# Strassen's seven half products in the MLP up projection of a fused decoder layer

## The chip, the cores and the metric

The kernel runs on one core of a Trainium2 chip. The core has five engines that the profile names PE (TensorE: matrix products), DVE (VectorE), ACT (ScalarE), POOL (GpSimd) and SP (SyncE, which here only issues DMAs). Each engine executes its own queue strictly in order; engines wait for each other by semaphores. The metric is the device time of one execution in microseconds (us). Three runs of the kernel before gave 668.95, 668.95 and 672.06 us.

## The reference

One decoder layer on a sequence of 512 tokens of width 1024, in float32: a mixer of two attention groups, then a squared-ReLU MLP with a hidden width of 4096, then a final RMSNorm. The change concerns the MLP alone:

```python
D_MODEL = 1024; SEQ = 512; D_FF = 4 * D_MODEL

def squared_relu_mlp(h, w_up, w_down):
    return jnp.square(jax.nn.relu(h @ w_up)) @ w_down

        h = h + squared_relu_mlp(rmsnorm(h, g_mlp[l]), w_up[l], w_down[l])
    return rmsnorm(h, g_final)
```

## The kernel before

A float32 product is made of three TensorE products of TensorE's 32-bit type fp32r. Each operand x is split into a high half xh (an fp32r copy, made on ACT) and a low half xl = x - xh (a subtraction on DVE); the function `mm3` (L189 to L192) then issues `lh*rh`, `ll*rh` and `lh*rl` into the same PSUM bank. The first operand of a matmul is the stationary one (a 128x128 block, loaded ahead by LDWEIGHTS, which the profile calls PEld), the second is the moving one. The printed rows name the moving one and then the stationary one: `S<-uh,wh` multiplies moving `uh` into stationary `wh` and adds into PSUM tile `S`. The PSUM tiles that the MLP uses are called S, T, O and acc.

The MLP input, normalised but for its row scale, lies transposed in SBUF as `uh`/`ul` (8 row blocks `kt` of 128 features, 512 tokens each). The 4096 hidden features are worked off in 8 blocks, e = 0 to 7, of 512 features, each in two halves:

- Up half: for each of four groups f of 128 features, `up_mm` (L1071) issues 8 kt x 3 = 24 matmuls that move 512 columns (tokens), so 96 in all. After each group follow a ReLU on ACT into `mt` (L1139), a square on ACT into the fp32r tile `ah` (L1140), the same square in full precision on POOL into `ma` (L1141), and `al = ma - ah` on DVE (L1142).
- Down half: for each of the four token groups tb and two column halves, 4 f x 3 = 12 matmuls of 512 columns, 96 in all. Stationary are blocks of `ah`/`al`, moving are the down weights. DVE adds each result to the residual `h1` (L1156). In the first token group (tb = 0) the groups f are taken as (0, 1, 2) for both column halves and then (3,).

The weights come from DRAM in pieces of 512 KB (128x1024, tile `wr`), issued by SP, and are split by `Ring`: ACT copies `wh` (L164), DVE subtracts `wl` (L118). Two sets of buffers exist: `ring`, whose tiles lie at the upper end of SBUF and are 512 wide, and `ring2`, at the lower end, 1024 wide; of each nine pieces three go to `ring` and six to `ring2`, so a projection's operands lie partly at one end and partly at the other. The right-hand pools put, counted in bytes of a partition, `uh`/`ul` at 143K and 160K, `h1` at 180K, `ring`'s halves at 204K to 229K; on the left lie `ring2`'s halves (35K to 84K) and `ah`/`al` (88K to 121K).

In block e = 0 three of the four up groups are begun early, while the last transposes of the input (`mlp_in`, four of them) are still being made. POOL has nothing else to do there.

The order of PE's queue is that of the code. The order on ACT, DVE, POOL and SP is laid down ahead of the run by a list scheduler over the whole program; on the chip it is fixed.

Of the kernel before, what the change touches and what calls it, by code (L numbers as in the profile page):

```python
# [15 lines left out]
P = 128  # L16
D = 1024
# [36 lines left out]
def hybrid_layer(tc, x, xT, wp, wfg, cst, gfin, out):  # L54
# [134 lines left out]
    def mm3(ps, lh, ll, rh, rl, first, last):  # L189
        nc.tensor.matmul(ps, lh, rh, start=first, stop=False)  # L190
        nc.tensor.matmul(ps, ll, rh, start=False, stop=False)  # L191
        nc.tensor.matmul(ps, lh, rl, start=False, stop=last)  # L192
# [855 lines left out]
    close_pool("att", "foxv")  # L1048
    hp = open_pool("hp", "right")
    h1 = hp.tile([P, NT, D], F32, name="h1")  # L1050
    ssh = cp.tile([P, NT, 2], F32, name="ssh")
    up = open_pool("up", "right")
    uh = up.tile([P, NK, S], F32R, name="uh")
    ul = up.tile([P, NK, S], F32R, name="ul")

    def wout_evac(ps, tb, half):
        cols = slice(512 * half, 512 * half + 512)
        nc.vector.scalar_tensor_tensor(h1[:, tb, cols], ps, rf[:, tb:tb + 1], fc["xr"][:, tb, cols], op0=ALU.mult, op1=ALU.add)
        jk = up.tile([P, S], F32, tag="jk", name=nm("jk"), bufs=2)
        nc.scalar.activation(jk, h1[:, tb, cols], AF.Square, accum_out=ssh[:, tb, half:half + 1])  # L1060
# [50 lines left out]
    gfb = mp.tile([P, D], F32, name="gfb")  # L1111
    nc.sync.dma_start(gfb, gfin.to_broadcast([P, D]))
# [10 lines left out]
    def nbank():  # L1123
        un[0] += 1
        return bank(tags[un[0] % 8])

    for e in range(8):
        ah = mp.tile([P, 4, S], F32R, tag="ah", name=nm("ah"), bufs=2)
        al = mp.tile([P, 4, S], F32R, tag="al", name=nm("al"), bufs=2)
        for f in range(4):  # L1130
            if early:
                w, ps = early.pop(0)
                up_mm(ps, w, range(4, NK))
            else:
                w, ps = mlp_piece(), nbank()
                up_mm(ps, w, range(NK))
            t = mp.tile([P, S], F32, tag="mt", name=nm("mt"), bufs=2)
            a = mp.tile([P, S], F32, tag="ma", name=nm("ma"), bufs=2)
            nc.scalar.activation(t, ps, AF.Relu)  # L1139
            nc.scalar.activation(ah[:, f, :], t, AF.Square)  # L1140
            nc.gpsimd.tensor_tensor(a, t, t, op=ALU.mult)  # L1141
            nc.vector.tensor_sub(al[:, f, :], a, f32(ah[:, f, :]))  # L1142
        wd = [mlp_piece() for _ in range(4)]
        for tb in range(NT):
# [35 lines left out]
    close_pool("up", "hp", "ringA", "edge", "mp", "ring2", "cp")  # L1180


def _pieces(w_in, w1k, w1v, w_out, w_up, w_down):
# [97 lines left out]
```

## Time and profile before

| | us |
|---|---|
| three runs | 668.95, 668.95, 672.06 |
| median | 668.95 |
| profiled execution | 669.01 |
| its span, first to last instruction | 667.2 |
| PE busy in the span | 650.7 (98%) |
| DVE busy | 405.6 (61%) |
| ACT busy | 312.8 (47%) |
| POOL busy | 170.6 (26%) |

The profiled execution is within 0.1 us of the median, and 1.8 us of it lie outside the span. Matmuls are pipelined: a row of 512 columns has a duration of about 0.39 us, but the next starts some 0.23 us later, so a step is read from start to start. The up half of block 0 begins, in part, at 306 us, its down half at 330.13 us, and the last matmul of the MLP starts at 659.76 us. Block 1 onwards fills the stretch from 352 to 660 us.

### The profile page before, as it was taken

How to read it: one execution, taken by the hardware profiler on the slowest of the kernel's cores; microseconds unless marked ns; L12 is line 12 of the kernel's file. 1: busy time of each engine (PE TensorE's matmuls, PEld its weight loads, DVE VectorE, ACT ScalarE, POOL GpSimd, SP SyncE). 2: the span in 40 equal slices, each digit the busy share in tenths (PEclk: the TensorE clock that was granted, in tenths of full speed). 3: DMA queues.
4: the chain of work that ended last, by engine and by line, in shares of the span. 5: the costliest groups of instructions: out<-in, count | busy, mean ns of one | idle time of the engine just before them, and what ended most of it. 6: DMA issues, size and time to landing. Idle time of an engine off the chain costs nothing.

```text
span 667.2 us, 9167 instructions
## 1 busy us (share of the span) xinstructions
PE 650.7 (98%) x3165; PEld 535.6 (80%) x3165; DVE 405.6 (61%) x872; ACT 312.8 (47%) x673; POOL 170.6 (26%) x203
## 2 busy tenths in 40 slices
PE   9998999999999999999999999999999999999995
PEld 7767888878787878888888888888888888888884
DVE  4798887868866789847936344354344433544146
ACT  5435536777867878637704223143142340422222
POOL 0262062655756745200301101001011020010121
PEclk9999999999999999999999999999999999999999
DMA  7723610000022573225814214143051330401002
GB/s 273 232 96 127 213 71 33 2 33 32 32 88 65 146 219 88 71 88 168 292 45 164 90 58 157 38 150 104 1 190 63 107 114 32 158 1 32 0 33 94
DMA packets 22878, 66.72 MB, mean 100 GB/s; under 512 B 4272, under 2 KB 4912, under 8 KB 22832
## 3 DMA queue, kind: packets, MB, share of 16 engines
q1 hardware_dynamic: 22688, 66.10, 29.4%
q8 instruction: 25, 0.41, 0.2%
q14 instruction: 21, 0.17, 0.1%
q10 hardware_dynamic: 144, 0.04, 0.0%
HBM read 59.81 MB, written 2.10 MB: 93 GB/s over the span
## 4 chain that ended last, share of the span: by engine, by line
PE 86%; DVE 8%; issue 2%; DMA 2%; ACT 1%; SPq 0%; POOL 0%; DVEq 0%; ACTq 0%
PE S L192 8%; PE S L190 8%; PE S L191 8%; PE acc L190 6%; PE acc L192 6%; PE acc L191 6%; PE O L190 5%; PE O L192 5%; PE O L191 5%; PE T L190 5%; PE T L192 5%; PE T L191 5%; PE O L756 4%; PE T L738 4%; PE S L710 2%
## 5 line engine op out<-in xcount | busy, mean ns | idle before, releaser
L164 ACT ACTIVATE wh<-wr 128x512 fp32r<-128x512 f32 (+1 forms) x144 | 103.5, 743 | 157.6 <-PE O L191 59.0
L118 DVE TENSOR_TENSOR wl<-wr,wh 128x512 fp32r<-128x512 f32 (+1 forms) x126 | 119.9, 971 | 93.5 <-ACT wh L164 91.6
L1141 POOL TENSOR_TENSOR ma<-mt 128x512 f32<-128x512 f32 x32 | 35.7, 1115 | 326.7 <-ACT mt L1139 326.7
L720 ACT ACTIVATE sp<-sp,st 128x128 f32<-128x128 f32 (+1 forms) x96 | 53.2, 555 | 16.9 <-DVE st L718 16.4
L718 DVE CUSTOM_DVE_ANT_0 sp<-S,c 128x128 f32<-128x128 f32 (+1 forms) x96 | 43.0, 485 | 18.7 <-PE S L711 18.2
L726 POOL TENSOR_SCALAR sp<-sp,st,gt 128x128 f32<-128x128 f32 (+1 forms) x64 | 38.5, 614 | 47.0 <-ACT sp L720 26.7
L118 DVE TENSOR_TENSOR ptl<-T,pth 128x128 fp32r<-128x128 f32 (+1 forms) x96 | 44.3, 483 | 2.9 <-ACT pth L748 2.5
L748 ACT ACTIVATE pth<-T 128x128 fp32r<-128x128 f32 (+1 forms) x96 | 38.5, 426 | 9.8 <-PE T L738 9.2
L738 PE MATMUL T<-c,sp 128*128 128x128 f32 x240 | 38.4, 273 | 3.1 <-DVE st L724 1.9
L738 PEld LDWEIGHTS T<-c,sp 128*128 128x128 f32 x240 | 29.6, 140 | 13.1 <-issue 5.1
L190 PE MATMUL S<-wh,ah 128*128 128x512 f32 (+1 forms) x100 | 38.9, 389 | 0.0
L192 PE MATMUL S<-wl,ah 128*128 128x512 f32 (+1 forms) x100 | 38.7, 387 | 0.0
L191 PE MATMUL S<-wh,al 128*128 128x512 f32 (+1 forms) x100 | 38.6, 386 | 0.0
L1156 DVE SCALAR_TENSOR_TENSOR h<-S,r2s,h 128x512 f32<-128x512 f32 (+1 forms) x25 | 18.5, 740 | 32.7 <-PE S L192 32.7
L190 PE MATMUL S<-uh,wh 128*128 128x512 f32 x88 | 34.6, 394 | 0.0
L192 PE MATMUL S<-ul,wh 128*128 128x512 f32 x88 | 34.4, 391 | 0.0
L191 PE MATMUL S<-uh,wl 128*128 128x512 f32 x88 | 34.2, 389 | 0.0
L1142 DVE TENSOR_TENSOR al<-ma,ah 128x512 fp32r<-128x512 f32 x32 | 21.8, 682 | 19.4 <-POOL ma L1141 19.4
L190 PE MATMUL acc<-xh,wh 128*128 128x512 f32 x72 | 30.9, 430 | 0.0
L192 PE MATMUL acc<-xl,wh 128*128 128x512 f32 x72 | 28.5, 395 | 0.0
L191 PE MATMUL acc<-xh,wl 128*128 128x512 f32 x72 | 28.4, 395 | 0.0
L190 PE MATMUL O<-uh,wh 128*128 128x512 f32 x72 | 28.4, 394 | 0.0
(349 smaller groups left out, 1690.3 us busy)
## 6 DMA issues: line engine op xcount, KB each, us to landing
wr<-wp_d SPq DMA_DIRECT2D x91, 512.0 KB, 3.7
wx<-wp_d SPq DMA_DIRECT2D x10, 512.0 KB, 4.2
xr<-x_d SPq DMA_DIRECT2D x4, 512.0 KB, 7.3
out_d<-ob SPq DMA_DIRECT2D x8, 256.0 KB, 2.1
xr<-xT_d SPq DMA_DIRECT2D x3, 512.0 KB, 6.6
fq<-tqh SPq DMA_DIRECT2D x8, 128.0 KB, 4.0
fq<-tq SPq DMA_DIRECT2D x8, 128.0 KB, 3.4
f2q<-tqh SPq DMA_DIRECT2D x8, 128.0 KB, 3.1
```

Source lines behind the costliest of these rows:

```text
L118: eng.tensor_tensor(o, a, b, op=ALU.subtract)
L164: high = lambda: nc.scalar.activation(hi, raw[:, c], AF.Copy)
L190: nc.tensor.matmul(ps, lh, rh, start=first, stop=False)
L191: nc.tensor.matmul(ps, ll, rh, start=False, stop=False)
L192: nc.tensor.matmul(ps, lh, rl, start=False, stop=last)
L718: nc.vector.tensor_tensor_reduce(out=self.p[i], in0=self.ps[i], in1=self.bias(i), scale=1.0, scalar=1e35, op0=ALU.add, op1=ALU.min, accum_ ...
L720: nc.scalar.activation(self.p[i], self.p[i], AF.Exp, bias=m, scale=-1.0, accum_out=den)
L726: nc.gpsimd.tensor_scalar(self.p[i], self.p[i], rs, g, op0=ALU.mult, op1=ALU.mult)
L738: nc.tensor.transpose(pt[:, j * P:j * P + P], self.p[i][:, j * P:j * P + P], ident)
L748: nc.scalar.activation(self.blocks(self.th, i), self.pt[i], AF.Copy)
L756: nc.tensor.matmul(o[:, j * P:S], self.v(j), t[:, 4 * j * P:(3 * j + NT) * P], start=first and part == 0 and j == 0, stop=last and part == ...
L1141: nc.gpsimd.tensor_tensor(a, t, t, op=ALU.mult)
```

## The change

Blocks e = 1 to 7 compute the up half in another way. The weight block W of 1024x512 is seen as 2x2 quarters: a11 and a12 belong to the hidden groups f = 0 and 2, a21 and a22 to f = 1 and 3; the second index is the half of the 1024 input features. The input is seen as 2x2 quarters too: u11, u12 (first 512 features, tokens 0 to 255 and 256 to 511), u21, u22. Instead of eight quarter products, seven are made, of sums of quarters (Strassen's scheme in Winograd's form):

P1 = a11 u11, P2 = (a21+a22)(u12-u11), P3 = (a21+a22-a11)(u22-u12+u11), P4 = a12 u21, P5 = (a11-a21)(u22-u12), P6 = (a12-(a21+a22-a11)) u22, P7 = a22 (u21-(u22-u12+u11)), the last two with their quarters as the kernel stores them.

Each product takes 2 x 4 x 3 = 24 matmuls of 256 columns, so a block has 168 of 256 columns where there were 96 of 512. P1, P3, P5 and P7 accumulate in one bank; ACT copies what stands in it after P1 (`e1`) and after P3 (`ev`), and P2 (`w5`); DVE adds three times (L1210). The weight sums (L1219 and three subtractions) are made on DVE, 1024 wide. The seven factors are then split in halves 512 wide, all in `ring`'s buffers (six of `wh`, six of `wl`: three products).

The four sums of the input are made once, in block 0 (`input_sums`, four calls, code placed in its down half): per call two additions of 512 columns and two subtractions of 256 on POOL (L1153, L118), two subtractions of 256 and two splits on DVE, two copies on ACT (L1159, L1162). They go to `tqh`/`tql`, and the fourth overwrites columns 256 to 511 of `uh`/`ul`.

Further: `ah`/`al` have one buffer in place of two; in the down half's first token group the groups f are taken as (0, 2) and then (1, 3); the down weights all come from `ring2` (four buffers, split 1024 wide), the up weights all from `ring`; the right-hand pools are opened in another order. As a result `uh` lies at 139K, `ul` at 155K, `tqh` and `tql` at 172K and 184K, `ring` at 204K to 229K, and `h1` at 123K; `ring2`'s halves at 52K to 84K, `ah` at 84.6K and `al` at 92.8K. The number of DMAs and their size stay as they were. In block 7 `gfb` and `ob` use raw weight tiles.

The diff, cut to its core:

```diff
-    hp = open_pool("hp", "right")
-    h1 = hp.tile([P, NT, D], F32, name="h1")
     up = open_pool("up", "right")
     uh = up.tile([P, NK, S], F32R, name="uh")
     ul = up.tile([P, NK, S], F32R, name="ul")
+    tqh = up.tile([P, 4, 3, 256], F32R, name="tqh")
+    tql = up.tile([P, 4, 3, 256], F32R, name="tql")
+    hp = open_pool("hp", "right")
+    h1 = hp.tile([P, NT, D], F32, name="h1")
...
-    ring2 = Ring(r2p, 6, 3, 1)
-    def mlp_piece():
-        return (ring if next_piece[0] % 9 < 3 else ring2).piece()
+    ring2 = Ring(r2p, 4, 7, 1)
...
+    def split2(r):
+        w = ([], [])
+        for k in range(2):
+            c = slice(512 * k, 512 * k + 512)
+            hi = rp.tile([P, 512], F32R, tag="wh", name=nm("wh"), bufs=6)
+            lo = rp.tile([P, 512], F32R, tag="wl", name=nm("wl"), bufs=6)
+            nc.scalar.activation(hi, r[:, c], AF.Copy)
+            sub(nc.vector, lo, r[:, c], f32(hi))
...
+    def input_sums(j):
+        r = raw().rearrange("p (k t) -> p k t", k=2)
+        t = raw().rearrange("p (a t) -> p a t", a=4)
+        for k in range(2):
+            nc.gpsimd.tensor_tensor(r[:, k], f32(uh[:, j + 4 * k, :]), f32(ul[:, j + 4 * k, :]), op=ALU.add)
+        u11, u12, u21, u22 = r[:, 0, 0:256], r[:, 0, 256:512], r[:, 1, 0:256], r[:, 1, 256:512]
+        sub(nc.gpsimd, t[:, 0], u12, u11)
+        sub(nc.gpsimd, t[:, 1], u22, t[:, 0])
+        sub(nc.vector, t[:, 2], u22, u12)
+        sub(nc.vector, t[:, 3], u21, t[:, 1])
+        nc.scalar.activation(tqh[:, j], t[:, 0:3], AF.Copy)
+        sub(nc.vector, tql[:, j], t[:, 0:3], f32(tqh[:, j]))
+        nc.scalar.activation(uh[:, j, 256:512], t[:, 3], AF.Copy)
+        sub(nc.vector, ul[:, j, 256:512], t[:, 3], f32(uh[:, j, 256:512]))
...
+    def product(ps, w, moving, first):
+        for p in range(2):
+            for j in range(4):
+                c = slice(P * j, P * j + P)
+                mm3(ps[:, 256 * p:256 * p + 256], w[0][p][:, c], w[1][p][:, c], moving(0, j), moving(1, j),
+                    first and p == j == 0, p == 1 and j == 3, skip_group_check=True)
...
-        ah = mp.tile([P, 4, S], F32R, tag="ah", name=nm("ah"), bufs=2)
-        al = mp.tile([P, 4, S], F32R, tag="al", name=nm("al"), bufs=2)
+        ah = mp.tile([P, 4, S], F32R, tag="ah", name=nm("ah"))
+        al = mp.tile([P, 4, S], F32R, tag="al", name=nm("al"))
...
+            product(pa, split2(a11), lambda h, j: u_in(h, j, 0), True)
+            e1 = half_copy("e1", pa)
+            a21, a22 = up_raw(), up_raw()
+            s1 = raw()
+            nc.vector.tensor_tensor(s1, a21, a22, op=ALU.add)
+            product(pd, split2(s1), lambda h, j: (tqh, tql)[h][:, j, 0], True)
+            w5 = half_copy("w5", pd)
+            sub(nc.vector, s1, s1, a11)
+            product(pa, split2(s1), lambda h, j: (tqh, tql)[h][:, j, 1], False)
+            ev = half_copy("ev", pa)
+            a12 = up_raw()
+            product(pc, split2(a12), lambda h, j: u_in(h, j + 4, 0), True)
+            hidden(ah, al, at(0, 0), add(pc, e1))
+            sub(nc.vector, a21, a11, a21)
+            product(pa, split2(a21), lambda h, j: (tqh, tql)[h][:, j, 2], False)
+            hidden(ah, al, at(1, 1), add(pa, w5))
+            sub(nc.vector, s1, a12, s1)
+            product(pd, split2(s1), lambda h, j: u_in(h, j + 4, 1), False)
+            hidden(ah, al, at(0, 1), add(pd, ev))
+            product(pa, split2(a22), lambda h, j: u_in(h, j, 1), False)
+            hidden(ah, al, at(1, 0), pa)
-        wd = [mlp_piece() for _ in range(4)]
+        wd = [ring2.piece() for _ in range(4)]
...
-            for fs in ((0, 1, 2), (3,)) if tb == 0 else ((0, 1, 2, 3),):
+            for fs in ((0, 2), (1, 3)) if tb == 0 else ((0, 1, 2, 3),):
...
+            if e == 0:
+                input_sums(tb)
```

What the scheduler makes of it is seen at three places. The first is POOL's whole queue around block 0. Before, after an instruction of the attention (`sq`), the four squares of block 0 stand alone:

```order
L783 TENSOR_TENSOR sq_3445<-sq_3445,sq_3294 128x512
L1141 TENSOR_TENSOR ma_3852<-mt_3851 128x512
L1141 TENSOR_TENSOR ma_3870<-mt_3869 128x512
L1141 TENSOR_TENSOR ma_3888<-mt_3887 128x512
L1141 TENSOR_TENSOR ma_3925<-mt_3924 128x512
```

In the changed kernel (`wr_...` are raw tiles that hold the sums, L1187 are the squares; eleven more sums stand above the first row):

```order
L118 TENSOR_TENSOR wr_4057<-wr_4056 128x256
L118 TENSOR_TENSOR wr_4057<-wr_4056,wr_4057 128x256
L1153 TENSOR_TENSOR wr_4096<-uh,ul 128x512
L1187 TENSOR_TENSOR ma_3844<-mt_3843 128x512
L1153 TENSOR_TENSOR wr_4096<-uh,ul 128x512
L118 TENSOR_TENSOR wr_4097<-wr_4096 128x256
L118 TENSOR_TENSOR wr_4097<-wr_4096,wr_4097 128x256
L1187 TENSOR_TENSOR ma_3862<-mt_3861 128x512
L1187 TENSOR_TENSOR ma_3880<-mt_3879 128x512
L1187 TENSOR_TENSOR ma_3921<-mt_3920 128x512
```

All sixteen sums of the input now stand ahead of the second, third and fourth square of block 0, thirteen of them ahead of the first too. The second place is DVE at the end of block 2's up half (`us` are the additions to a product, `wl` low halves of weights, `al` those of the hidden features). Before:

```order
L1142 TENSOR_TENSOR al_4365<-ma_4402,ah_4364 128x512
L118 TENSOR_TENSOR wl_4745<-wr_4742,wh_4744 128x512
L118 TENSOR_TENSOR wl_4749<-wr_4742,wh_4748 128x512
L1142 TENSOR_TENSOR al_4365<-ma_4443,ah_4364 128x512
L118 TENSOR_TENSOR wl_4786<-wr_4783,wh_4785 128x512
L118 TENSOR_TENSOR wl_4790<-wr_4783,wh_4789 128x512
L1142 TENSOR_TENSOR al_4365<-ma_4484,ah_4364 128x512
L118 TENSOR_TENSOR wl_4827<-wr_4824,wh_4826 128x1024
L1142 TENSOR_TENSOR al_4365<-ma_4521,ah_4364 128x512
L1156 SCALAR_TENSOR_TENSOR h_3566<-T_4550,r2s,h_3566 128x512
```

In the changed kernel:

```order
L1210 TENSOR_TENSOR us_4715<-O_4526,w_968_4602 128x512
L118 TENSOR_TENSOR wl_4949<-wr_4942,wh_4948 128x512
L118 TENSOR_TENSOR wl_4985<-wr_4982,wh_4984 128x512
L1210 TENSOR_TENSOR us_4756<-S_4527,ev_4637 128x512
L118 TENSOR_TENSOR al_4525<-ma_4718,ah_4524 128x2x256
L118 TENSOR_TENSOR wl_4989<-wr_4982,wh_4988 128x512
L118 TENSOR_TENSOR wr_4982<-wr_4982,wr_4942 128x1024
L118 TENSOR_TENSOR al_4525<-ma_4759,ah_4524 128x2x256
L118 TENSOR_TENSOR wl_5020<-wr_4982,wh_5019 128x512
L118 TENSOR_TENSOR al_4525<-ma_4797,ah_4524 128x2x256
```

Six rows of the next block's weights (P1 to P3 of block 3: `wr_4942` is its a11, `wr_4982` its sum) now stand between the additions and the low halves of this block's hidden features; the last `al` has the first of P3's `wl` directly ahead of it. The third place is PE where a down half begins (block 3 in the changed kernel, block 2 in the one before; the numbers of `wh` count the groups f in steps of 6, so that 4528 is f = 0 and 4546 f = 3, and 5218 and 5236 likewise). Before, from its 16th matmul on:

```order
L190 MATMUL S_4551<-wh_4540,ah_4364 128x512
L191 MATMUL S_4551<-wh_4540,al_4365 128x512
L192 MATMUL S_4551<-wl_4541,ah_4364 128x512
L190 MATMUL T_4550<-wh_4546,ah_4364 128x512
L191 MATMUL T_4550<-wh_4546,al_4365 128x512
L192 MATMUL T_4550<-wl_4547,ah_4364 128x512
```

In the changed kernel, from its 10th on:

```order
L190 MATMUL acc_5241<-wh_5230,ah_4938 128x512
L191 MATMUL acc_5241<-wh_5230,al_4939 128x512
L192 MATMUL acc_5241<-wl_5231,ah_4938 128x512
L190 MATMUL S_5240<-wh_5224,ah_4938 128x512
L191 MATMUL S_5240<-wh_5224,al_4939 128x512
L192 MATMUL S_5240<-wl_5225,ah_4938 128x512
L190 MATMUL S_5240<-wh_5236,ah_4938 128x512
L191 MATMUL S_5240<-wh_5236,al_4939 128x512
```

Before, the group that is made last, f = 3, is used from the 19th matmul of the down half on. Now f = 0 and 2 fill the first 12 matmuls, and f = 1 and 3 are used from the 13th and the 16th on; their first 256 tokens are what P7, the last product, completes.

## Rows read from the trace of the kernel before

**Rows 1.** The page: engines' busy time, and the granted clock by fortieths of the span.

```profile
PE 650.7 (98%) x3165; PEld 535.6 (80%) x3165; DVE 405.6 (61%) x872; ACT 312.8 (47%) x673; POOL 170.6 (26%) x203
PEclk9999999999999999999999999999999999999999
```

**Rows 2.** The page: the chain that ended last, shares by engine.

```profile
PE 86%; DVE 8%; issue 2%; DMA 2%; ACT 1%; SPq 0%; POOL 0%; DVEq 0%; ACTq 0%
```

**Rows 3.** By windows: us; busy PE, PEld, DVE, ACT, POOL; clock; DMA share, GB/s.

```profile
480.00:520.00 40.00, 40.00 (x176) 32.81 (x175) 18.23 (x21) 12.69 (x18) 4.17 (x4) 1.00 0.31 105
```

**Rows 4.** Timeline of PE (start, duration, us): first matmuls of up and down halves.

```profile
330.13 0.39 PE L190 MATMUL T<-wh,ah 128*128 128x512 f32 x1
...
352.26 0.39 PE L190 MATMUL T<-uh,wh 128*128 128x512 f32 x1
...
374.14 0.39 PE L190 MATMUL S<-wh,ah 128*128 128x512 f32 x1
...
395.91 0.39 PE L190 MATMUL S<-uh,wh 128*128 128x512 f32 x1
...
505.06 0.39 PE L190 MATMUL T<-wh,ah 128*128 128x512 f32 x1
...
527.25 0.40 PE L190 MATMUL T<-uh,wh 128*128 128x512 f32 x1
...
615.55 0.40 PE L190 MATMUL T<-uh,wh 128*128 128x512 f32 x1
...
637.53 0.40 PE L190 MATMUL S<-wh,ah 128*128 128x512 f32 x1
```

**Rows 5.** Timeline of PE at the MLP's end: 512 columns, then 256.

```profile
649.82 0.40 PE L192 MATMUL T<-wl,ah 128*128 128x512 f32 x1
...
657.02 0.28 PE L190 MATMUL O<-wh,ah 128*128 128x256 f32 x1
...
659.76 0.28 PE L192 MATMUL S<-wl,ah 128*128 128x256 f32 x1
```

**Rows 6.** Timeline of weight loads under the steps of 256 columns.

```profile
657.14 0.19 PEld L192 LDWEIGHTS O<-wl,ah 128*128 128x128 f32 x1
657.26 0.19 PEld L190 LDWEIGHTS O<-wh,ah 128*128 128x128 f32 x1
```

**Rows 7.** Lines by form, DVE, 470 to 660 us: count; busy, mean ns; idle before.

```profile
L118 DVE TENSOR_TENSOR wl<-wr,wh 128x1024 fp32r<-128x1024 f32 x18 | 21.8, 1223 | 33.8 <-ACT wh L164 33.8
L1142 DVE TENSOR_TENSOR al<-ma,ah 128x512 fp32r<-128x512 f32 x16 | 11.0, 685 | 19.4 <-POOL ma L1141 19.4
L1156 DVE SCALAR_TENSOR_TENSOR h<-S,r2s,h 128x512 f32<-128x512 f32 x14 | 10.5, 750 | 17.6 <-PE S L192 17.6
```

**Rows 8.** Lines by form, ACT, the same stretch.

```profile
L164 ACT ACTIVATE wh<-wr 128x1024 fp32r<-128x1024 f32 x18 | 18.5, 1052 | 20.5 <-PE O L191 17.8 <-DMA wr<-wp_d 2.6
L1139 ACT ACTIVATE mt<-S 128x512 f32<-128x512 f32 x6 | 3.6, 599 | 19.0 <-PE S L192 19.0
```

**Rows 9.** Timeline of POOL and DVE where one meets the other's work.

```profile
500.56 1.04 POOL L1141 TENSOR_TENSOR ma<-mt 128x512 f32<-128x512 f32 x1 [4.41 <-ACT mt L1139]
501.03 1.12 DVE L118 TENSOR_TENSOR wl<-wr,wh 128x512 fp32r<-128x512 f32 x1 [2.57 <-ACT wh L164]
502.07 0.68 DVE L1142 TENSOR_TENSOR al<-ma,ah 128x512 fp32r<-128x512 f32 x1
...
326.61 2.03 POOL L1141 TENSOR_TENSOR ma<-mt 128x512 f32<-128x512 f32 x1 [1.16 <-ACT mt L1139]
326.53 2.66 DVE L118 TENSOR_TENSOR wl<-wr,wh 128x1024 fp32r<-128x1024 f32 x2
```

**Rows 10.** Lines by form, POOL, whole span: operations with two tiles as operands.

```profile
L783 POOL TENSOR_TENSOR sq<-sq,sq 128x512 f32<-128x512 f32 x4 | 5.2, 1291 | 2.2 <-ACT sq L778 2.2
L670 POOL TENSOR_TENSOR cs<-cs,cm 128x256 f32<-128x256 f32 x4 | 2.8, 710 | 1.2 <-DVE cm L669 1.1
```

**Rows 11.** Timeline of DVE: the fifth of the input's eight low halves.

```profile
310.49 0.75 DVE L1067 SCALAR_TENSOR_TENSOR ul<-T,c,uh 128x512 fp32r<-128x512 f32 x1 [0.72 <-ACT uh L1066]
```

More of the change, by code (lines that the diff above doesn't have):

```diff
@@ L187, in part, with mm3 @@
         return w[0][k][:, c:c + n], w[1][k][:, c:c + n]
[L189 to L192, printed above, removed]
+    def mm3(ps, lh, ll, rh, rl, first, last, **kw):
+        nc.tensor.matmul(ps, lh, rh, start=first, stop=False, **kw)
+        nc.tensor.matmul(ps, ll, rh, start=False, stop=False, **kw)
+        nc.tensor.matmul(ps, lh, rl, start=False, stop=last, **kw)
     def rsqrt(ss, scale, n, rname):
@@ L1125, in nbank, with raw @@
         return bank(tags[un[0] % 8])
-    for e in range(8):
-        ah = mp.tile([P, 4, S], F32R, tag="ah", name=nm("ah"), bufs=2)
-        al = mp.tile([P, 4, S], F32R, tag="al", name=nm("al"), bufs=2)
[L1130 to L1142, printed above, removed]
-        wd = [mlp_piece() for _ in range(4)]
+    def raw():
+        return r2p.tile([P, 1024], F32, tag="wr", name=nm("wr"), bufs=7)
@@ new lines, in u_in, with half_copy @@
+    def u_in(h, j, half):
+        return (uh, ul)[h][:, j, 256 * half:256 * half + 256]
+    def product(ps, w, moving, first):
[4 more added lines that the diff above has]
+                    first and p == j == 0, p == 1 and j == 3, skip_group_check=True)
+    def half_copy(n, ps):
+        t = mp.tile([P, S], F32, tag=n, name=nm(n))
+        nc.scalar.activation(t, ps, AF.Copy)
+        return t
@@ L1151, in hybrid_layer @@
                         mm3(ps, ah[:, f, tok], al[:, f, tok], *part(wd[f], c, n), f == 0, f == 3)
+            if e == 0:
+                input_sums(tb)
             last = groups[-1]
-            ob = mp.tile([P, D], F32, tag="ob", name=nm("ob"), bufs=2) if e == 7 else None
+            ob = raw() if e == 7 else None
+            if e == 7 and tb == 0:
+                gfb = raw()
+                nc.sync.dma_start(gfb, gfin.to_broadcast([P, D]))
             for i, (ps, (c, n)) in enumerate(zip(pss, groups)):
@@ L1206, in _pieces @@
     for e in range(8):
-        for f in range(4):
-            c = (4 * e + f) * P
-            ps += kmajor(w_up[:, c:c + P])
+        up = [kmajor(w_up[:, (4 * e + f) * P:(4 * e + f + 1) * P])[0] for f in range(4)]
+        if e > 0:
+            up = [np.concatenate([up[i][:, 512 * k:512 * k + 512], up[i + 2][:, 512 * k:512 * k + 512]], 1)
+                  for i, k in ((0, 0), (1, 0), (1, 1), (0, 1))]
+        ps += up
         ps += [w_down[(4 * e + f) * P:(4 * e + f + 1) * P] for f in range(4)]
```

47 lines of the change are left out of this document (39 added, 8 removed).

## The prediction

> **What bounds the kernel now.** I read the page first: PE is busy for 650.7 of 667.2 us at the full clock (a 9 in every slice) [rows 1], and the chain that ended last is PE for 86% [rows 2]. By windows, a stretch of the MLP shows it pure: in 40 us PE is never idle, DVE works 18.2 us, ACT 12.7, POOL 4.2 [rows 3]. So in the MLP time is the number of matmul steps times their length, as long as nobody is late; and DVE, the busiest helper, has more than half of its time free. The third view is PE's timeline. An up half takes 21.88 us (352.26 to 374.14) or 21.98 (615.55 to 637.53), a down half 21.77 (374.14 to 395.91) or 22.19 (505.06 to 527.25) [rows 4]; with 96 steps each that is 227 to 231 ns a step. Steps of 256 columns stand at the end: 23 of them from 657.02 to 659.76 are 119.1 ns each, against 232.3 for the 31 steps of 512 before them (649.82 to 657.02) [rows 5]. Half the width costs 51%, so nearly no fixed price hangs on a step.
>
> **The products.** Seven blocks give up 96 steps of 512 and get 168 of 256. At 119.1 ns that is 20.0 us against 21.9: 1.9 less. The same tiles that read 119.1 read 232.3 at 512, 2% above the 228 of an up half, so I scale to 118.5: 19.9 us, 2.0 less, **-14.0 us** in seven blocks (with 119.5 it is -12.8; with 117, half of 228 and 3 ns, -15.7). PE's own work lies on the path, so this counts in full where PE doesn't wait.
>
> What a page says against it: by the Trainium skill, "TensorE: Matmul & The Clock Gate", section "The mechanism" of Part 3, a weight load overlaps a running matmul only where the two use different row groups of the array, and here all use all 128 rows. In the trace two loads of 0.19 us start 0.12 us apart while the matmuls keep their 119 ns [rows 6]; so the trace disagrees. By the page the added loads would be paid, and the sum would be that of the last rival.
>
> **The placement.** Two kinds of down half stand in the trace: 21.77 us in block 1, but 22.13 in block 0 (330.13 to 352.26) and 22.19 in block 4 [rows 4]. What differs is in which buffers the weights lie. With all down weights beside `ah`/`al` I expect the short kind, about 0.4 less in two to three of seven blocks, **-1.0 us**. The bounds are the same 0.4 either way in most blocks, -2.0 to +1.0: that the new places are the better ones no row shows.
>
> **Block 0, which now makes the input's sums.** Before, POOL has only four squares there. Now thirteen of sixteen sums stand ahead of the first square and three ahead of the second. The second addition needs the fifth low half, done at 310.49 + 0.75 = 311.2 [rows 11]. From there to the second square's start POOL has 7 additions (1.29), 8 subtractions (at most 0.71) [rows 10] and a square (1.04 alone [rows 9]): 15.7 us, so about 327.0. The rest goes through three engines in order. POOL's second square ends at 328.1; DVE makes `al` of f = 1 (0.69 [rows 7]) and the subtractions that its queue holds behind it (estimate 0.35 each, half of 512 columns), 329.4; ACT copies a sum of 768 columns (estimate 0.8, between 0.6 for 512 and 1.05 for 1024 [rows 8]) before the ReLU of f = 2 (0.60 [rows 8]), 330.8; POOL's square 331.9, `al` 332.6. The down half starts at 330.13 [rows 4] and, in the new order, wants `al` of f = 2 at its 5th matmul, 331.0: 1.6 late. Then the ReLU of f = 3 waits on ACT behind four copies of 256 columns, one of 768 and two high halves of 512, and its `al` on DVE behind three low halves of 256, one of 768, two of weights and a weight sum: some 4 us, so 336.9 against a need at 333.8 (the 17th matmul). **+3.1 us**, if POOL and DVE don't disturb each other.
>
> But they do. A subtraction of 512 columns that met POOL's square took 1.12 us in place of 0.69, and a square that met DVE's 1024-wide subtractions took 2.03 in place of 1.04 [rows 9]. If half of the sixteen operations ahead of the second square meet one, at up to 1.0 each, up to 8 us more; DVE is occupied about half of this stretch by operations on SBUF, the additions being longer than a square. I take 3 more: **+6.1 us** (1 to 11; no gain, since before nothing waited there).
>
> **The six full blocks after it.** The down half now wants f = 1 at its 13th matmul, so 12 x 0.227 = 2.7 us after its start, 22.6 us after the block's. Two chains end there. The short one begins at P7's end: ReLU 0.1 + 0.6, square 1.04 + 0.07, `al` 0.69: 2.5 us, it would just do. The other is DVE's queue. From the first down weight it lists, up to that `al`: 7 operations of 1024 (four `wl` of down weights, three weight sums), 17 of 512 in SBUF (13 `wl`, 4 `al`), 4 that read PSUM. Following each other they take 0.08 less than their durations (502.07 against 501.03 + 1.12 [rows 9]): 7 x 1.14 + 17 x 0.61 + 4 x 0.67 [rows 7, 9] = 21.1. The first can start 0.9 us before the block does: its buffer's last reader is nine steps from the down half's end (-2.0), and ACT's copy takes 1.05 [rows 8]. So there are 23.5 us. Four meetings with POOL's squares at 0.43 (1.12 less 0.69 [rows 9]) make 22.8, and waits for high halves come on top, since ACT can make a `wh` only when PE has left a buffer: two or three of 0.5, half a copy of 1.05 [rows 8], say 1.4. That is 24.2, 0.7 late. The last `al` also stands behind a `wl` of the next block, whose `wh` waits for a 1024-wide sum two rows above. I take 0.7 a block, six blocks (behind block 7 no weights follow): **+4.2 us** (0 to 1.5 each, 0 to 9). Who waits: PE alone, and all the down half behind it.
>
> **Nothing for the rest.** The DMAs are as many and as large. P7's start and the additions wait for DVE within the chain above. Block 7's `gfb` is loaded later but used only after the first down sums. The tail behind 659.76 keeps its instructions. Two buffers of `ah` become one: P4 writes it after the down half before has ended long since.
>
> **Sum**, on the profiled execution of 669.0 us (0.1 above the median): -14.0 - 1.0 + 6.1 + 4.2 = -4.7, **664.3 us**.
>
> **The rivals.**
> *Meetings cost little* (0.25). What speaks for it: only 0.43 us were lost on DVE in the one meeting [rows 9], and the queues may find room for it. Then block 0 costs 3.1 and the others at most 0.1: 669.0 - 15.0 + 3.1 + 0.6 = 657.7; with the lowest prices 655.
> *The gain is eaten* (0.18). POOL and DVE exclude each other: at 501.03 DVE ran for 1.12 us of which the first 0.43 lie within POOL's square, as if it had waited for its end, and POOL's 2.03 fits a wait for one 1024-wide operation [rows 9]. If so throughout, block 0 costs about 9 and each later block 1.0: 669.0 - 15.0 + 9 + 6 = 669.0, no change. The Trainium skill, "SBUF — State Buffer", section "SBUF: two separate sides", has this as a rule: the port pair that VectorE and GpSimd share is an exclusive lock, held for a whole instruction, when a VectorE instruction with two SBUF inputs meets a GpSimd one that reads SBUF. The first meeting agrees with it (1.12 us); the last only in part, since DVE's two operations there took 2.66 us, 0.3 more than 1.22 + 1.14, where a whole square of 1.04 would have been due.
> *DVE becomes the bound of the up half* (0.09). The up half shrinks by 2 us while DVE's list grows to 21 us of 23.5. It decides from 2.3 us of waiting per block on: then six blocks lose what they gained. For it speaks that each `wl` waits for ACT's `wh` and ACT's queue mixes ReLUs, copies and the next block's halves in fixed order: two or three more waits of a whole copy (1.05) are 2.6 us on top of 0.7: 669.0 - 15.0 + 6.1 + 6 x 3.3 = 680, slower. Against it: DVE is idle over 50% of the stretch now [rows 3].
> *Loads show* (0.01): if no load overlapped, 72 more of 0.19 us [rows 6] would be paid in each of seven blocks, 96 us: 669.0 - 15.0 + 96 = 750; that a load of the same length already stands at each step of 119 ns speaks against it. That the products aren't all made cannot be: PE's queue holds 504 matmuls more, 7 x 72.
>
> **How the numbers follow.** The forecast has 0.47, its own range is 661 to 668. A bound of 0.5%, 3.3 us, is about what a measurement of this kernel can tell from no change: faster is under 665.6, slower over 672.3. Of the forecast's 0.47 two thirds lie under 665.6 (0.31), the rest is the same; with the second case faster has 0.56, the same 0.16 + 0.15 = 0.31, slower 0.03 of the third, 0.09 and 0.01. The range leaves out the slower cases and the lower tail of the first rival: 656 to 671.
>
> **What would show it.** In PE's timeline after: P1 to P7 in 19.9 us; a gap of 4 to 8 us within the first 20 matmuls of block 0's down half, released by `al` and `ah`; 0.5 to 1 us before the 13th or 14th matmul of the six next down halves, none in block 7; all down halves but for the gap 21.8 us. POOL's additions over 1.29 us mean that meetings cost. The prediction is wrong if steps of 256 columns are over 125 ns, if PE waits inside the products (then DVE or ACT is the bound), or if no gap stands in block 0.

## The result

The changed kernel takes 685.11 us (median of four runs, 684.72 to 687.05) against 668.95 us: a ratio of 1.0236, 95% interval 1.02 to 1.0272. It is slower by 16 us; the prediction said 664.3 and had 671 as the upper end of its range.

The page of the kernel after, the lines that answer to [rows 1] and [rows 2], and the slices of the clock:

```profile
PE 645.2 (94%) x3669; PEld 552.3 (81%) x3669; DVE 503.5 (74%) x987; ACT 356.1 (52%) x752; POOL 195.1 (29%) x219
...
PEclk9999999999999999999899999999999999999998
...
PE 61%; DVE 18%; ACT 6%; DMA 5%; issue 5%; POOL 3%; SPq 0%; DVEq 0%; ACTq 0%; POOLq 0%
```

PE is busy 5.5 us less, and its share falls from 98% to 94%. In the chain that ended last PE went from 86% to 61% and DVE from 8% to 18%. The span grew from 667.2 to 682.9 us, 15.7 more. PE's timeline at the block borders (start, duration; first matmuls, as [rows 4]) says where:

```profile
332.72 0.39 PE L190 MATMUL T<-wh,ah 128*128 128x512 f32 x1
...
364.54 0.28 PE L190 MATMUL T<-uh,wh 128*128 128x256 f32 x1
...
384.92 0.40 PE L190 MATMUL O<-wh,ah 128*128 128x512 f32 x1
...
409.06 0.28 PE L190 MATMUL O<-uh,wh 128*128 128x256 f32 x1
...
429.70 0.40 PE L190 MATMUL S<-wh,ah 128*128 128x512 f32 x1
...
455.47 0.28 PE L190 MATMUL S<-uh,wh 128*128 128x256 f32 x1
...
653.63 0.40 PE L190 MATMUL T<-wh,ah 128*128 128x512 f32 x1
```

| part | before | after | difference |
|---|---|---|---|
| up to the start of block 1 | 352.26 | 364.54 | +12.3 |
| seven up halves, blocks 1 to 7 | 153.4 | 142.6 | -10.8 |
| six down halves, blocks 1 to 6 | 131.9 | 146.5 | +14.6 |
| block 7's down half and the tail | 29.7 | 29.3 | -0.4 |

Each row is read from first matmul to first matmul. An up half now takes 20.15 to 20.7 us, a down half 24.1 to 24.2 (25.77 in block 2) where one without waits takes 21.79 (as the third experiment shows): 2.36 us are lost. The idle times in brackets below add up to only 1.8 of them, since they count from the end of a matmul, and a next one could have started before that. Why the down halves wait shows in block 2, in PE's and then in DVE's, ACT's and POOL's timeline ahead of its 13th matmul (last column: idle before, and the releaser):

```profile
434.11 0.49 PE L190 MATMUL S<-wh,ah 128*128 128x512 f32 x1 [1.49 <-ACT ah L1186]
434.91 0.50 PE L191 MATMUL S<-wh,al 128*128 128x512 f32 x1 [0.31 <-DVE al L118]
...
418.72 1.23 DVE L1219 TENSOR_TENSOR wr<-wr,wr 128x1024 f32<-128x1024 f32 x1 [0.86 <-DMA wr<-wp_d]
...
424.30 1.11 DVE L118 TENSOR_TENSOR wl<-wr,wh 128x512 fp32r<-128x512 f32 x1 [0.68 <-ACT wh L1136]
...
429.36 1.53 DVE L118 TENSOR_TENSOR wl<-wr,wh 128x512 fp32r<-128x512 f32 x1
430.93 1.95 DVE L118 TENSOR_TENSOR wr<-wr,wr 128x1024 f32<-128x1024 f32 x1
432.80 0.68 DVE L118 TENSOR_TENSOR al<-ma,ah 128x512 fp32r<-128x512 f32 x1
...
429.96 0.60 ACT L1185 ACTIVATE mt<-O 128x512 f32<-128x512 f32 x1 [0.15 <-PE O L192]
432.90 0.63 ACT L1136 ACTIVATE wh<-wr 128x512 fp32r<-128x512 f32 x1 [2.34 <-DVE wr L118]
433.44 0.61 ACT L1186 ACTIVATE ah<-mt 128x512 fp32r<-128x512 f32 x1
...
429.22 1.12 POOL L1187 TENSOR_TENSOR ma<-mt 128x512 f32<-128x512 f32 x1 [0.50 <-ACT mt L1185]
430.64 1.15 POOL L1187 TENSOR_TENSOR ma<-mt 128x512 f32<-128x512 f32 x1 [0.30 <-ACT mt L1185]
```

POOL's square starts at 429.22, DVE's `wl` 0.14 us later takes 1.53 in place of 0.69. The next square starts at 430.64, the next block's weight sum 0.29 later takes 1.95 in place of 1.23. ACT has made the ReLU of P7 by 430.56 and then idles for 2.34 us: next in its queue is the `wh` of that sum, and `ah`, for which PE waits, stands behind it. Earlier in the block a `wl` lost 0.43 us in the same way (424.30), and DVE stood idle for 0.86 us until a piece of the next block's weights had landed (418.72); both count below.

Block 0 shows the same on a larger scale. POOL's timeline, then DVE's, while the sums of the input are made:

```profile
316.22 2.31 POOL L1153 TENSOR_TENSOR wr<-uh,ul 128x512 f32<-128x512 f32 x1 [0.76 <-DVE r2s L1111]
...
321.31 3.56 POOL L1153 TENSOR_TENSOR wr<-uh,ul 128x512 f32<-128x512 f32 x2
324.83 1.71 POOL L118 TENSOR_TENSOR wr<-wr 128x256 f32<-128x256 f32 x1
...
334.02 1.75 POOL L1187 TENSOR_TENSOR ma<-mt 128x512 f32<-128x512 f32 x1
...
313.56 1.25 DVE L204 TENSOR_SCALAR rt<-rt 128x4 f32<-128x4 f32 x1
...
317.27 0.74 DVE L1071 SCALAR_TENSOR_TENSOR ul<-T,c,uh 128x512 fp32r<-128x512 f32 x1
...
321.34 4.60 DVE L118 TENSOR_TENSOR wl<-wr,wh 128x1024 fp32r<-128x1024 f32 x2
```

Two weight halves of 1024 took 4.60 us in place of 2.36, two additions 3.56 in place of 2.58 [rows 10]. PE waits 1.69 and 0.73 us for a late `ul` already in the up half. In the down half it waits 5.55 us for `ah` and 0.67 for `al` of f = 2 (4th and 5th matmul), and 1.10 for `al` of f = 3 (17th). (Ten sums, not eleven, stand above the first row of POOL's queue as printed ahead of the prediction; thirteen ahead of the first square is right.)

A third loss is the clock. The windows at block 0's long wait and in block 2 (the granted clock, 1.00 when full, is the third number from the end):

```profile
333.60:337.00 3.40, 0.00 (x0) 0.00 (x0) 2.47 (x4) 0.07 (x1) 2.17 (x2) 1.00 0.00 0
337.20:343.80 6.60, 4.00 (x9) 2.81 (x10) 6.60 (x11) 5.68 (x12) 2.80 (x2) 0.50 0.76 241
...
436.00:439.00 3.00, 3.00 (x9) 2.31 (x8) 1.38 (x2) 0.00 (x0) 0.00 (x0) 0.51 0.00 0
```

In block 0 the clock fell during the wait of 5.55 us, in block 2 after waits of 1.49 and 0.31, each time to half, the level of 1.2 GHz: steps of 512 columns are 0.43 us apart in place of 0.23. In block 2 that is the 1.6 us by which its down half exceeds the other five, which had the same waits and kept the clock.

### The profile page after: what moved, and what is told of

Same layout as the page of the kernel before. It is cut to its first block, busy times and chain, and to the rows that moved or that the text cites. A ratio compares the mean times of both kernels' runs of the same rounds, so it can differ in the third digit from the quotient of the medians.

```text
span 682.9 us, 10322 instructions
## 1 busy us (share of the span) xinstructions
PE 645.2 (94%) x3669; PEld 552.3 (81%) x3669; DVE 503.5 (74%) x987; ACT 356.1 (52%) x752; POOL 195.1 (29%) x219
## 4 chain that ended last, share of the span: by engine, by line
PE 61%; DVE 18%; ACT 6%; DMA 5%; issue 5%; POOL 3%; SPq 0%; DVEq 0%; ACTq 0%; POOLq 0%
DVE wl L118 6%; PE acc L190 5%; PE S L192 5%; PE acc L191 5%; PE acc L192 5%; PE S L191 5%; PE S L190 5%; PE O L756 4%; PE T L738 4%; PE O L191 3%; PE O L192 3%; PE O L190 3%; DMA wr<-wp_d 3%; PE T L191 3%; PE T L192 3%
## 5 line engine op out<-in xcount | busy, mean ns | idle before, releaser
L118 DVE TENSOR_TENSOR wl<-wr,wh 128x512 fp32r<-128x512 f32 (+1 forms) x176 | 153.3, 896 | 27.2 <-ACT wh L164 15.1
L164 ACT ACTIVATE wh<-wr 128x512 fp32r<-128x512 f32 (+1 forms) x96 | 69.6, 765 | 131.5 <-PE T L191 36.0
L1187 POOL TENSOR_TENSOR ma<-mt 128x512 f32<-128x512 f32 x32 | 38.1, 1191 | 284.7 <-ACT mt L1185 284.7
L1136 ACT ACTIVATE wh<-wr 128x512 fp32r<-128x512 f32 x98 | 60.7, 624 | 36.6 <-DVE wr L118 17.6
L118 DVE TENSOR_TENSOR ptl<-T,pth 128x128 fp32r<-128x128 f32 (+1 forms) x96 | 44.3, 483 | 2.9 <-ACT pth L748 2.5
L118 DVE TENSOR_TENSOR wr<-wr,wr 128x1024 f32<-128x1024 f32 (+1 forms) x25 | 33.1, 1323 | 0.7
L190 PE MATMUL T<-wh,ah 128*128 128x512 f32 (+1 forms) x68 | 26.7, 393 | 5.6 <-ACT ah L1186 5.6
L118 DVE TENSOR_TENSOR al<-ma,ah 128x512 fp32r<-128x512 f32 x32 | 23.0, 719 | 8.8 <-POOL ma L1187 8.8
L190 PE MATMUL S<-uh,wh 128*128 128x256 f32 (+1 forms) x96 | 28.3, 295 | 0.3 <-DVE us L1210 0.3
L190 PE MATMUL O<-wh,ah 128*128 128x512 f32 x64 | 25.6, 400 | 3.0 <-ACT ah L1186 3.0
```

What stands on the lines that cost most here:

```text
L118: eng.tensor_tensor(o, a, b, op=ALU.subtract)
L164: high = lambda: nc.scalar.activation(hi, raw[:, c], AF.Copy)
L190: nc.tensor.matmul(ps, lh, rh, start=first, stop=False, **kw)
L1136: nc.scalar.activation(hi, r[:, c], AF.Copy)
```

## The experiments

The theory after this reading: POOL's and DVE's operations on SBUF shut each other out (one waits while the other runs; below this is called the exclusion), and this, not the amount of DVE's work, makes block 0 and the six down halves late. The rivals: DVE's and ACT's order alone does it, or the new order of the groups f. The runs without an interval below are single ones; runs of the kernel before gave 668.4 to 673.03 us.

**Without the sums of the input.**

```diff
             if e == 0:
-                input_sums(tb)
+                for t, u in ((tqh, uh), (tql, ul)):
+                    nc.scalar.activation(t[:, tb], f32(u[:, 2 * tb:2 * tb + 2, 0:384]), AF.Copy)
```

> The sums of the input are left out: ACT fills tqh/tql with plain copies of uh/ul, so four of the seven products multiply other data (same shapes, same number of matmuls). Theory A (block 0 is late because POOL's and DVE's sums hold up its squares and low halves): the up half of block 0 ends near 330 us again, its down half takes 22 to 23 us in place of 31.8, the time falls by 11 to 12.5 us to about 673. Rival B (block 0 is late because of the new order (0, 2), (1, 3) and the fewer buffers): at least 4 of the 12 us stay, about 677 or more. Both: blocks 1 to 7 as in the changed kernel, 2.3 us of waiting at the start of six down halves.

Measured: 674.51 us, 10.6 less, a little under the 11 to 12.5 expected. Block 0's down half starts at 330.02 and takes 23.3 us; the six later ones wait as before. So the sums cost nearly all of block 0's 12.3: block 1 starts at 353.35, 1.1 us later than in the kernel before, after waits of 0.24 and 0.76 us for f = 3, which the new order wants earlier. Theory A holds, rival B accounts for a tenth. This run takes POOL's and DVE's share of the sums away together, so it doesn't tell the exclusion from the amount of work.

**Squares on ACT.**

```diff
-        nc.gpsimd.tensor_tensor(a, t, t, op=ALU.mult)
+        if e == 0:
+            nc.gpsimd.tensor_tensor(a, t, t, op=ALU.mult)
+        else:
+            nc.scalar.activation(a, t, AF.Square)
```

> In blocks 1 to 7 the square in full precision (ma) is made by ACT in place of POOL; POOL is then idle there. Theory A (the 2.3 us per down half come from POOL's squares and DVE's two-operand work shutting each other out): the two DVE operations ahead of the last al fall from 1.53 and 1.95 us to 0.7 and 1.23, the wait at the 13th matmul from 1.65 + 0.6 to 0.5 to 1 us, the time by 6 x 1.3 to 6 x 1.8, to 674 to 677. Rival B (DVE's list and ACT's order alone make it late, the next block's weight sum stands ahead): the wait stays at 1.8 us or more, since ACT has 0.5 us more for each of four squares; time 682 to 687.

Measured: 671.70 us, 13.4 less, more than expected. DVE's timeline at the same place of block 2 has the same operations in the same order:

```profile
425.69 0.69 DVE L118 TENSOR_TENSOR wl<-wr,wh 128x512 fp32r<-128x512 f32 x1
426.41 1.22 DVE L118 TENSOR_TENSOR wr<-wr,wr 128x1024 f32<-128x1024 f32 x1
427.55 0.68 DVE L118 TENSOR_TENSOR al<-ma,ah 128x512 fp32r<-128x512 f32 x1
```

0.69 and 1.22 us in place of 1.53 and 1.95; the down halves take 22.2 to 23.1 us in place of 24.15, and the clock stays up in block 2. Over the stretch from 365 to 640 us the lines by form (count; busy, mean ns; idle before) have the weight sums of the changed kernel

```profile
L118 DVE TENSOR_TENSOR wr<-wr,wr 128x1024 f32<-128x1024 f32 x18 | 26.4, 1465 | 0.6
```

and of this one:

```profile
L118 DVE TENSOR_TENSOR wr<-wr,wr 128x1024 f32<-128x1024 f32 x18 | 22.1, 1225 | 0.6
```

So the exclusion is the larger part of the 2.36 us per block: 0.8 us a block (0.5 to 1.3) are left when it is gone. That is the part of DVE's list, of ACT's order and of the pieces of weights that DVE waits for (0.2 to 1.1 us a block in this run too).

**The down half in the order of the products.** Four PSUM banks are opened at a time:

```diff
+        if e > 0:
+            opened = {tb: [nbank(), nbank()] for tb in (0, 2)}
+            for tb, fs, first in ((0, (0, 2), True), (2, (1, 3), True), (2, (0, 2), False), (0, (1, 3), False)):
+                down(opened[tb], tb, two, fs, first, not first)
+        for tb in range(NT) if e == 0 else (2, 0, 1, 3):
```

> The down half of blocks 1 to 7 takes its work in the order in which the products complete it: token group 0 with f = 0, 2 (P4), group 2 with f = 1, 3 (P5), group 2 with f = 0, 2 (P6), group 0 with f = 1, 3 (P7), then groups 1 and 3; four PSUM banks are open at a time. Theory A (only the last few al are late; DVE has room over the whole block, 28 of 40 us): the waits of 2.3 us vanish, and with them the fall of the clock in block 2: six down halves of 21.8 us, 685 - 14 - 1.6 = 669 to 671. Rival B (DVE as a whole is what the block waits for): the waits move into the next products, whose 20.2 us grow by 1 us or more each, and the time stays over 677.

Measured: 670.36 us, 14.7 less. The down halves wait for nothing: PE's timeline has 21.79 us for that of block 1, from 385.12 to 406.91, and the same for the next five:

```profile
385.12 0.40 PE L190 MATMUL O<-wh,ah 128*128 128x512 f32 x1
...
406.91 0.28 PE L190 MATMUL O<-uh,wh 128*128 128x256 f32 x1
```

The products didn't grow (20.15 to 20.7 us). DVE as a whole is no bound; only a few of its results came late, at one point. Theory A. The order has a price at the kernel's end: from the start of block 7's down half it takes 30.4 us (29.3 in the changed kernel), and in all the later runs with this order 30.4 to 30.5. Whether the old order in block 7 alone would save it was not tested.

**The placement alone, in the kernel before.**

```diff
-                w, ps = mlp_piece(), nbank()
+                w, ps = ring.piece(), nbank()
-        wd = [mlp_piece() for _ in range(4)]
+        wd = [ring2.piece() for _ in range(4)]
```

and the pool of `uh`/`ul` opened ahead of that of `h1`.

> The kernel before with the placement alone: all up weights in the buffers at the upper end, all down weights at the lower, the pool of uh/ul opened first; no products are changed. Theory A (the places set two kinds of down half, 21.8 and 22.2 us): all eight down halves take 21.8 us, up halves 21.8 to 21.9, 667.5 to 668.2. Rival B (the places do nothing, the two kinds have another cause): four long down halves stay, 669. Rival C (four up pieces per block in a ring with three come late): PE waits in the up halves, over 671.

Measured: 665.92 beside 669.53 us, 1.6 us under theory A's window, and again for an interval:

> The placement alone once more, now for an interval: all up weights at the upper end, all down weights at the lower, no product changed. One look gave 665.92 us beside 669.53. Theory A: the eight up and eight down halves are each about 0.1 and 0.3 us shorter, so 0.5% less, ratio 0.994 to 0.997. Rival B (a chance of that execution): ratio 0.998 to 1.002.

a ratio of 0.9958 (0.9939 to 0.9978). In PE's timeline of the first of the two runs every up half from block 1 on takes 21.80 us and every down half 21.77 (21.80 in block 7), 226.8 to 227.1 ns a step of 512 columns:

```profile
351.56 0.39 PE L190 MATMUL T<-uh,wh 128*128 128x512 f32 x1
...
373.36 0.39 PE L190 MATMUL S<-wh,ah 128*128 128x512 f32 x1
...
395.13 0.39 PE L190 MATMUL S<-uh,wh 128*128 128x512 f32 x1
```

So the placement is a gain of its own, about 3 us. In that trace 1.7 of them are in the down halves of blocks 1 to 7, 0.8 in the up halves and 0.7 ahead of block 1; the last is not in the second trace, where PE waits 0.15 and 0.12 us in block 0. It also takes away from the products: beside 21.8 us, an up half of 20.15 saves 1.65.

**The sums on DVE in block 0.** `nc.gpsimd` becomes `nc.vector` in the four lines of `input_sums`.

> The changed kernel with all sixteen sums of the input on DVE, none on POOL, at the same place in the code. Theory A (the price of block 0 is the exclusion: 18 us of POOL's work and DVE's work one after the other): the work on DVE grows by about 10 us, POOL's 18 us go, and block 0 loses 3 to 5 us against the kernel before in place of 12; time 676 to 678. Rival B (it is the amount of work ahead of the low halves, on whatever engine): block 0 still loses 8 us or more, 681 or more.

Measured: 676.49 us. Block 0's down half starts on time and takes 24.56 us in place of 31.82: block 0 costs 2.3 us and not 12.3, less than the 3 to 5 expected, although DVE has all the work. By the balance of block 0 theory A is right. But block 1 pays 3.8 us: its P7 waits 1.4 us and its down half takes 26.6, 1.6 of which are the half clock, which falls here and not in block 2. The late P7 is not DVE's amount of work: DVE's timeline has it idle in block 1, at the weight sum of the next block, for 2.35 us (0.61 in the changed kernel) until a piece of weights has landed, and the additions that P7 needs stand behind that sum.

**The sums in block 1, and the order of the products.** Blocks 0 and 1 in the old form, seven products in six blocks; a copy of one column of `al` into the sums' tile keeps DVE from making them in block 0:

```diff
+        nc.vector.tensor_copy(r[:, 0, 0:1], f32(al[:, j, 0:1]))
         for k in range(2):
-            nc.gpsimd.tensor_tensor(r[:, k], f32(uh[:, j + 4 * k, :]), f32(ul[:, j + 4 * k, :]), op=ALU.add)
+            nc.vector.tensor_tensor(r[:, k], f32(uh[:, j + 4 * k, :]), f32(ul[:, j + 4 * k, :]), op=ALU.add)
```

> Blocks 0 and 1 in the old form, seven products in blocks 2 to 7 only, all sums of the input on DVE and tied behind the low halves of block 1; the down half in the order of the products (as in the run on the token order). Theory A (nothing but the waits and the first block ate the gain): block 0 as before, 22 us down; six blocks give 1.65 us each (20.15 in place of 21.80 us, both at the new places) and the placement 3.1 to 3.6: 669.0 - 3.4 - 9.9 = 655 to 656. Rival B (the sums only move their price into block 1, where DVE gets 15 us more): PE waits in block 1 or in P2 of block 2, over 658.

Measured: 662.62 us, ratio 0.9877 (0.984 to 0.9914): faster than the kernel before, but 7 us over what was expected. Blocks 0 and 1 are clean, so rival B is not the cause. P7 waits for DVE in three of six blocks, worst in block 6 (PE's timeline; then DVE's in block 6 and, twice, in block 4):

```profile
585.27 0.36 PE L190 MATMUL T<-uh,wh 128*128 128x256 f32 x1 [1.53 <-DVE us L1211]
...
576.96 1.23 DVE L1220 TENSOR_TENSOR wr<-wr,wr 128x1024 f32<-128x1024 f32 x1 [1.85 <-DMA wr<-wp_d]
...
490.03 1.23 DVE L1220 TENSOR_TENSOR wr<-wr,wr 128x1024 f32<-128x1024 f32 x1 [0.46 <-DMA wr<-wp_d]
...
495.60 1.11 DVE L118 TENSOR_TENSOR wl<-wr,wh 128x512 fp32r<-128x512 f32 x1 [0.68 <-ACT wh L1136]
```

A `wl` two rows ahead of that addition took 1.11 us in place of 0.69: again a square. The expectation had wrongly taken the exclusion for harmless once the down half had slack. But a square isn't enough: the same 1.11 us stand in block 4 (495.60), where PE doesn't wait. What differs is the weight sum of the next block (L1220), which stands ahead of the addition in DVE's queue. DVE is idle there until a piece of weights has landed: 1.53, 1.95 and 1.85 us in blocks 2, 5 and 6, in which P7 waits, and 0.30 and 0.46 in blocks 3 and 4, in which it doesn't. Why the pieces came late was not tested.

**The same with squares on ACT.**

> The late sums and the token order together, and the squares of blocks 2 to 7 on ACT, so that POOL is idle there. Theory A (what is left of waiting, 0.2 to 0.5 us before P7 in every second block, is DVE held up by POOL's squares): these waits go, 1 to 2 us less than the same kernel with POOL's squares. Rival B (they come from DVE's list or ACT): no change within 0.5 us, or slower because ACT has four squares more per block.

Measured: 658.27 us, ratio 0.982 (0.9788 to 0.9852), 4.3 us less than with POOL's squares, where 1 to 2 were expected. No PE wait over 0.2 us is left in the seven blocks after block 0, up halves take 20.15 (21.80 in block 1, which is in the old form) and down halves 21.8. Theory A again; how much of the 4.3 us is the meetings themselves and how much the pieces of weights, for which DVE now waits 0.6 to 1.1 us at most, is not separated. That no wait is left and the time is still 2 to 3 us over the 655 to 656 of the run before has in part to do with the kernel's end (1.1 us, as above) and with the stages before the MLP, which begins 0.7 us later. This is the kernel that beats both: 11 us less than before, 27 less than the change as it was made.

**Seven blocks after all, sums on DVE in block 0, products' order.**

> Seven products in blocks 1 to 7, the sums on DVE in block 0, the down half of block 0 in the old order (0, 1, 2), (3), that of the others in the order of the products. Theory A: one block more than the kernel with late sums gains 1.65 us, block 0 loses 2 to 4 us, so 656 to 658, 0 to 2 us more than the late sums. Rival B (DVE overflows in block 0 and P2 of block 1 is late too): over 660.

Measured: 662.57 us, ratio 0.9894 (0.9853 to 0.9934); 5 us over theory A and in rival B's range. Block 0's down half takes 23.87 us, 2.1 more than without the sums, and P7 of block 1 waits 3.07 (PE's timeline, then DVE's):

```profile
374.11 0.36 PE L190 MATMUL T<-uh,wh 128*128 128x256 f32 x1 [3.07 <-DVE us L1210]
...
366.55 1.23 DVE L1219 TENSOR_TENSOR wr<-wr,wr 128x1024 f32<-128x1024 f32 x1 [3.61 <-DMA wr<-wp_d]
```

So DVE doesn't overflow, as rival B had it: it is idle for 3.61 us until a piece of the next block's weights has landed, with the additions of this block behind it in its queue. With squares on ACT:

> Seven products in blocks 1 to 7, the sums on DVE in block 0, the down halves in the order of the products, and the squares of blocks 1 to 7 on ACT. Theory A (in block 1 DVE is short of time, and POOL's squares take the last of it): the 3.2 us before P7 of block 1 shrink to 1 to 2, block 0 loses 2, all other waits go: 657 to 659, level with the version that leaves block 1 in the old form. Rival B: the wait in block 1 is DVE's own work, and stays at 3 us: 659 to 661.

Measured: 660.53 us, ratio 0.9856 (0.9829 to 0.9882). The time is 1.5 us above theory A's window and in rival B's, but the wait before P7 of block 1 is 1.52 us, as theory A had it. Of the 1.55 us that went, 0.7 are three `wl` that took 2.05 us in place of 2.73 without a square beside them, and 0.6 an `al` that now stands behind the addition in DVE's queue. What is left is not DVE's own list, but again the late piece, for which DVE waits 3.31 us. In its profiled execution the MLP also began at 309.2 us, 3 us later than in the run before it. Nearly all of that came between 214 and 222 us, in the attention, with a wait of PE for a DMA and then the half clock (PE's timeline, then a window):

```profile
216.79 0.30 PE L710 MATMUL S<-fk,fq 128*128 128x128 f32 x1 [1.94 <-DMA f2q<-tqh]
...
218.00:221.50 3.50, 3.50 (x11) 2.65 (x10) 2.52 (x13) 2.46 (x9) 0.90 (x2) 0.51 0.44 101
```

That execution is the longest of the four (658.93 to 662.62 us), so it says nothing about the change. It doesn't beat the version that leaves block 1 in the old form; the intervals of the two ratios overlap.

## Why the prediction was wrong

**Products: direction right, size off.** -14.0 was said, -10.8 measured. A step is 119.9 ns (20.15 us for 168), not 118.5: the row at the MLP's end read 119.1, and scaling it down had no ground. That is 1.7 us of seven blocks. The rest, 1.5 us, are delays of up to 0.5 us before P7; they are longest in blocks 2, 4 and 6, where DVE had waited 0.86, 0.91 and 0.67 us for a piece of weights (0.34 to 0.61 in the others). The weight loads overlap, as the row said. The prediction had read one sentence of the Trainium skill, "TensorE: Matmul & The Clock Gate", section "The mechanism" of Part 3, against this. The same section of the Trainium skill also lets a load into the background weight buffer be pulled ahead of a running matmul. So it spoke less against the row than the prediction had it; which of the two cases stands here no run shows.

**Placement: direction right, too small.** -1.0 was said; alone it gives 3 us, because four down halves of blocks 1 to 7 gain 0.4 and not two or three, and because the up halves and block 0 gain too. In the changed kernel it is worth 1.1 in the six down halves, since the products replaced seven of the up halves.

**Block 0: the step that failed is the price of the meetings.** +6.1 was said, +12.3 measured, above the 11 that bounded it. The chain over POOL, DVE and ACT was the right one: PE waits for f = 2 and then for f = 3. But "half of the sixteen operations meet one" and "3 more" were too little: without meetings POOL's second square was to start at 327.0, and it started at 334.02 (its row stands with block 0 above), 7.0 later. POOL's and DVE's work ran nearly one after the other. What was not seen at all is the up half before it: short DVE operations and `ul` came late too, 2.6 us. The half clock after the wait added another 1.5 or so (six steps of 0.43 us and one of 0.59 in place of 0.23). The lower bound of 3.1 without meetings was not measured: 2.3 us with the sums on DVE are near it, but that is another chain, without POOL's sums.

**The six down halves: the step that failed is the room in DVE's list, and its waits above all.** +4.2 was said with 9 as the bound; 2.36 us in six blocks made 14.1, block 2's clock 1.6 more, and the placement took 1.1 back. The place was right (13th and 14th matmul, released by `ah` and `al`, none in block 7), and the meetings' sum was nearly right, by luck. "Four meetings at 0.43" are 1.7 us; in each of the six blocks three operations of DVE lost 0.43, 0.84 and 0.72, which is 2.0. A meeting isn't 0.43 us: that figure came from one row in which the subtraction began 0.47 us after the square, one that begins 0.14 after it loses 0.84, and one that begins 0.29 after it 0.72. Delay and loss add up to 0.9 to 1.0 us, nearly a square.

What was too small is the rest of the list. From the first `wl` of a down weight to the `al` for which PE waits it takes 26.2 to 26.8 us in the six blocks, where 24.2 was said. DVE's waits in it are 2.6 to 3.2 us and not 1.4: 1.7 for ACT's high halves, 0.3 to 0.9 for a piece of weights, which had been put at nothing ("the DMAs are as many and as large"), 0.3 for a square, and small gaps. Its own work is 21.6 and not 21.1 (the sum as printed gives 21.0). The longer up half gave back 0.2 to 0.8. So by the forecast's terms the list had 1.0 us to spare without meetings (21.1 + 1.4 of 23.5), and the meetings would first have used that up. With the squares on ACT the down halves are still 0.8 us late, so there was nothing to spare: of the 2.0 us of meetings 1.6 reach the down half. The squares come right after the ReLUs, when DVE is always at work, and the loss passes through `wh` to ACT's queue and to `ah`, at which PE stops first.

**The rivals.** "The gain is eaten" had the mechanism, at 9 us and 1.0 a block; it was 12.3 and 2.3. I gave it 0.18, because the row at 326.53, where DVE lost only 0.3 us, seemed to speak against a full exclusion. By the Trainium skill, "SBUF — State Buffer", section "SBUF: two separate sides", VectorE and GpSimd share a port pair that is locked for a whole instruction, among other cases when a VectorE instruction with two SBUF inputs meets a GpSimd one that reads SBUF. The runs agree with it (0.69 to 1.53 and 1.23 to 1.95 us beside a square, 0.69 and 1.22 without), and as a rule it was the better guide than the one row; that row, with 0.3 us lost, stays unexplained. "DVE becomes the bound of the up half" fell as to the place: with the order of the products changed PE waited 0.3 us at most there. But its 680 us came nearest to the measured time, and what it was built on, more waiting of DVE for ACT's high halves than 1.4 us held, is in part what the traces show.

## What to carry to other kernels

Before POOL is given work beside a busy DVE, add both durations on SBUF as if one engine did them, as an upper bound, and look for the place where a result of either is wanted soon; moving four squares per block to a half-idle ACT was worth 4 to 13 us here. When a scheme shortens a stage, order the consumer by when the pieces are finished before looking for faster engines: that alone took away 14 us of waiting. A queue in fixed order also carries a late piece of the next block's weights into work that is ready: look at what stands behind it. And try a bundled change in parts: its placement alone was a gain that the rest hid.

## What the hardware showed that was not expected

The exclusion takes in short operations and those with one operand: `rt<-rt` of 128x4 took 1.25 us beside POOL's additions, 0.17 before (its row stands with block 0 above). By the same section of the Trainium skill a VectorE instruction in a two-port mode takes the lock as well. Whether this one ran in it no run here shows. DVE's `ul` at 317.27, which reads PSUM, kept its 0.74 us in the middle of an addition of POOL's (316.22 to 318.53).

Where tiles lie sets the length of a step: 227 ns at the new places, up to 232 at the old [rows 5], for the same matmul at the full clock. Which of the places matters was not separated.

The granted clock fell to half during a wait of 5.55 us, and once after waits of 1.49 and 0.31 that five other blocks had without it. The length of a wait alone doesn't decide: before P7 of block 1 in the run with the sums on DVE and the products' order, PE waited 3.07 us and the clock stayed full. What decides stays open.
